# Moving the gates' small operations from the second expert's step to the end of the first expert's up-projection

## The chip, the cores and the metric

One core of one Trainium2 chip runs the program. The metric is the device time of one execution in microseconds (us). The kernel before takes 889.69 us, the median of three runs (887.64, 889.69 and 891.66).

## What is computed

One layer of a decoder trunk on 512 tokens of width 1024: an HGRN2 branch and a stick-breaking attention branch, mixed; a cross-attention to a memory of 256 rows; and a mixture of experts. Each of the three ends in a residual and a layer norm. All is float32 at the outside. The change lies in the last stage, the mixture of experts:

```python
g_prob = softmax(hf @ wg + bg);  g_top, g_idx = top_k(g_prob, 1)        # 1 of 4 groups
in_group = the 4 expert logits of that group
e_top, e_idx = top_k(softmax(in_group), 2)                              # 2 of 4 experts
gate_w = g_top * (e_top / sum(e_top))
for e in range(16):
    hidden = silu(hf @ w1[e]) * (hf @ w3[e])                            # 1024 -> 512
    y += combine[:, e:e+1] * (hidden @ w2[e])                           # 512 -> 1024
out = layer_norm(alpha * h + y)
```

`combine` holds `gate_w` at a token's two experts and zero elsewhere.

## The kernel before

**Stages.** The first two thirds of the span compute the two branches and the cross-attention, with float32 products split in three. The mixture of experts runs from about 596 us on. It does not multiply every token with every expert: the router gives each expert a list of slots, and each expert's weights (two of 1024 x 512 and one of 512 x 1024, 6.3 MB) are streamed once.

**One expert's step.** The loop over `e` issues, in this order: `up(e)`, the first two products for 64 slots, whose two halves run side by side in TensorE's columns (L1425), and a conditional part for slots 64 to 127 (L1412 to L1415, L1436), which TensorE's sequencer enters only if the count of tokens, loaded into a register at L1430, is over 64 or 96; `turn_in(e + 1)`, eight transposes (L1398) of the next expert's token rows, with two copies out of PSUM (L1399); the start of the gather for expert `e + 3` (L1161, on POOL's queue); for `e > 0` the second product of expert `e - 1`, `down(e - 1)` (L1466, with its own conditional part), the scaling of its result by the slots' gates in `to_rows` (L1489, L1495 on ScalarE, L1497 on VectorE), and the scatter that adds the rows to the sum in memory (L1273, POOL's queue); and `turn_hidden(e)`, four transposes of the hidden rows (L1453). Expert 0's second product is thus issued in the step of expert 1.

**Weights.** `Weights` (`W`) keeps a list of loads of 512 KB each, in order of use, and the free buffers. `W.done(j)` frees a buffer and at once issues the next load on SP's queue (L54); SP waits there until the buffer's last reader is through. In `up`, `W.done` stands behind the conditional part, so the eight buffers of an `up` are free for SP when TensorE's sequencer has passed the If at L1412. Buffers for some 40 loads make the stream run ahead of TensorE.

**Side work.** `begin(gen, wait)` puts a generator on a list; `tick()`, called after every pair of weights, lets it issue a part of its instructions once its waiting time is used up, and `finish()` issues all that is left. `tell()` (L1362) is begun before the loop and finished in `up(0)`: it counts the tokens, tells each slot its token (L1109, with one-hot matrices), starts the gathers for experts 1 and 2, and issues the first half of the gates' chain (`route_gates`, L1119: five VectorE operations, then two exponentials on ScalarE, L1133 and L1134). `tell_gates()` (L1375) is the rest: `route_gates_rest` with 12 small VectorE operations (L1139 to L1153), 24 bf16 products of 128 x 16 that sum each slot's gate (L1109) into the PSUM tile `told`, a copy (L1380), ten float32 products, 20 TensorE instructions (L1385), that move the gates to the partitions in which `to_rows` wants them, and a copy to `gates_at` (L1386). Before the change it is begun in step 0, behind `turn_in(1)`, so it is issued in the ticks of `up(1)` and of `down(0)`. `gates_at` is read first by `to_rows(0)`, at the end of `down(0)`.

Every engine works through its instructions in the order of issue.

Of the kernel before, what the change touches and what calls it, by code (L numbers as in the profile page):

```python
# [96 lines left out]
def tile_kernel(ctx, tc, x, mem, ln_in_g, ln_in_b, w_in, hg_lb_logits, hg_norm_g, w_branch_a, w_branch_b,  # L97
# [51 lines left out]
    def work(name, shape, dt=F32, bufs=2):  # L149
        return pp.tile(shape, dt, tag=name, bufs=bufs, name=nc.get_next_instruction_name() + name)  # L150
# [47 lines left out]
    def tick(n=1.0):  # L198
        for s in list(side):
            s[1] -= n  # L200
            while s[1] <= 0:
                try:
                    s[1] += next(s[0]) or 1
                except StopIteration:
                    side.remove(s)
                    break

    def begin(gen, wait=0):
        side.append([gen, wait])

    def finish(gen=None):
        while side:
            tick()
# [892 lines left out]
    def sums(o, items):  # L1106

        for i, (r, t, k) in enumerate(items):
            nc.tensor.matmul(o, oh_b[r][:, t], C[:, k, r, t], start=i == 0, stop=i == len(items) - 1)  # L1109
# [27 lines left out]
    def route_gates_rest():  # L1137
        L, top, tmp = logits, gexp[:, :, 4], gexp[:, :, 0:4]
        nc.vector.tensor_reduce(gates[:, 0, 0], tmp, op=ALU.add, axis=AX.X)  # L1139
        yield 0.35  # L1140
        nc.vector.scalar_tensor_tensor(gates[:, 0, 0], gates[:, 0, 1], 1.0, gates[:, 0, 0], op0=ALU.add, op1=ALU.mult)
        yield 0.35
        nc.vector.reciprocal(gates[:, 0, 0], gates[:, 0, 0])
        yield 0.35
        nc.vector.tensor_tensor(gates[:, 0, 1], gates[:, 0, 0], gates[:, 0, 1], op=ALU.mult)
        yield 0.35
        f = lambda x: x.rearrange("p r t -> p (r t)")
        for i in range(3):
            part = gparts[:, i]
            nc.vector.tensor_copy(part, f(gates[:, i]))  # L1150
            if i < 2:
                nc.vector.tensor_tensor(f(gates[:, i + 1]), f(gates[:, i]), part, op=ALU.subtract)
            nc.vector.tensor_tensor(C[:, 2 + i].rearrange("p r t e -> p (r t) e"), m.rearrange("p r t e -> p (r t) e"),  # L1153
                                    part[:, :, None].to_broadcast([P, 2 * NT, NE]), op=ALU.mult)
            yield 0.35
# [4 lines left out]
    def gather(e):  # L1160
        nc.gpsimd.indirect_dma_start(out=gx[e % 2], out_offset=None, in_=x2d[:, :],  # L1161
                                     in_offset=bass.IndirectOffsetOnAxis(ap=gidx[:, e:e + 1], axis=0),
                                     bounds_check=T - 1, oob_is_err=False)
# [101 lines left out]
    def more_blocks():  # L1265
        n = nc.values_load(more[0:1, 8:9], min_val=0, max_val=7)
        with tc.If(n > 0):
            list_blocks()
            with tc.For_i(0, n):
                one_block()  # L1270

    def scatter(y, idx):
        nc.gpsimd.indirect_dma_start(out=yd[:, :], out_offset=bass.IndirectOffsetOnAxis(ap=idx, axis=0),  # L1273
                                     in_=y, in_offset=None, bounds_check=T - 1,
                                     oob_is_err=False, compute_op=ALU.add)
# [99 lines left out]
    def tell_gates():  # L1375
        yield 0.5
        yield from route_gates_rest()
        yield 2
        sums(told[:, NE:2 * NE], [(r, t, k) for r, t in all_rt for k in range(2, 5)])
        nc.vector.tensor_copy(gate, told[:, NE:2 * NE])  # L1380
        yield 1

        for i, (s0, n) in enumerate(((0, 64), (64, 32), (96, 32))):
            for k in range(0, P, n):
                nc.tensor.matmul(told[k:k + n, (i + 2) * NE:(i + 3) * NE], ident[:, s0:s0 + n], gate, start=True, stop=True)  # L1385
        nc.vector.tensor_copy(gates_at, told[:, 2 * NE:5 * NE].rearrange("p (a e) -> p a e", e=NE))  # L1386
# [6 lines left out]
    def turn_in(e):  # L1393
        xg = gx[e % 2].rearrange("t (q p k) -> t q k p", q=4, k=2)
        for q in range(2):
            p = msp()
            for i in range(4):
                nc.tensor.transpose(p[:, i * P:(i + 1) * P], xg[:, 2 * q + i // 2, i % 2], ident)  # L1398
            (nc.scalar.copy, nc.vector.tensor_copy)[q](xgT[:, e % 2, 4 * q:4 * q + 4],  # L1399
                                                       p.rearrange("p (k n) -> p k n", n=P))  # L1400
# [9 lines left out]
    def further(e, part):  # L1410
        n = beyond[e]
        with tc.If(n > 64):  # L1412
            part(0)
            with tc.If(n > 96):
                part(1)  # L1415

    def up(e):
        x, (a, b) = xgT[:, e % 2], sums_up
        ws = []
        for q, js in enumerate(q_up[e]):  # L1420
            ws.append([W.get(j) for j in js])
            for k in range(2):
                c = 2 * q + k
                for i, w in enumerate(reversed(ws[q])):
                    nc.tensor.matmul(a[64 * i:64 * i + 64], x[:, c, 0:64], w[:, k * 512:(k + 1) * 512], start=c == 0,  # L1425
                                     stop=c == 7)
            tick()
        if e == 0:
            finish()
        beyond[e] = nc.tensor.value_load(tally[0:1, e:e + 1], min_val=0, max_val=T)  # L1430

        def part(g):
            for c in range(8):
                for i in range(4):
                    o = c % 2 * 512 + i % 2 * 256
                    nc.tensor.matmul(b[32 * i:32 * i + 32, 256 * g:256 * g + 256],  # L1436
                                     x[:, c, 64 + 32 * g:96 + 32 * g], ws[c // 2][i // 2][:, o:o + 256],
                                     start=c == 0, stop=c == 7)

        further(e, part)  # L1440
        for js in q_up[e]:
            for j in js:
                W.done(j)
        h = work("w2k", [P, T], bufs=5)
        for s, gated, other in ((slice(0, 64), a[64:128], a[0:64]), (slice(64, 128), b[0:64], b[64:128])):
            nc.scalar.activation(h[s], gated, AF.Silu)
            nc.vector.tensor_tensor(h[s], h[s], other, op=ALU.mult)
        return h

    def turn_hidden(e, h, p=None):  # L1450
        p = p or msp()
        for i in range(4):
            nc.tensor.transpose(p[:, i * P:(i + 1) * P], h[:, i * P:(i + 1) * P], ident)  # L1453
        x = work("w2k", [P, T], bufs=5)
        nc.vector.tensor_copy(x, p)  # L1455
        hT[e] = x.rearrange("p (k n) -> p k n", n=P)

    def down(e):

        x, (a, b) = hT.pop(e), sums_down  # L1460
        ws = [W.get(j) for j in q_w2[e]]

        def base():
            for k, w in enumerate(ws):
                for n in range(2):
                    nc.tensor.matmul(a[64 * n:64 * n + 64], x[:, k, 0:64], w[:, n * 512:(n + 1) * 512], start=k == 0,  # L1466
                                     stop=k == 3)
                tick()

        def part(g):  # L1470
            for k, w in enumerate(ws):
                s = slice(64 + 32 * (k // 2), 96 + 32 * (k // 2))
                for i in range(4):
                    nc.tensor.matmul(b[32 * i:32 * i + 32, 256 * g:256 * g + 256], x[:, 2 * g + k % 2, s],
                                     w[:, 256 * i:256 * i + 256], start=k == 0, stop=k == 3)

        def rest():
            further(e, part)
            for j in q_w2[e]:
                W.done(j)  # L1480

        return base, rest
# [17 lines left out]
    for e in range(NE - 1):  # L1500
        h = up(e)
        turn_in(e + 1)
        if e + 3 < NE:
            gather(e + 3)
        if e == 13:
            scratch.extend(W.raw_free.pop() for i in range(4))
            more_blocks()
            W.buffers(scratch)
        if e == 0:
            begin(tell_gates())  # L1510
        if e > 0:
            for step in down(e - 1):
                step()
            finish()
            scatter(to_rows(e - 1), gidx[:, e - 1:e])
        turn_hidden(e, h)
# [58 lines left out]
    ident_r = pp.tile([P, 3 * P], F32R, tag="hgc", name="ident_r")[:, 0:P]  # L1575
    nc.scalar.copy(ident_r, ident)
    h = up(NE - 1)
    for t in (1, 2):
        split_tile(t, rooms.pop())
# [115 lines left out]
```

## Time and profile before

| | |
|---|---|
| median of three runs | 889.69 us |
| profiled execution, whole | 890.44 us |
| its span | 888.3 us |
| TensorE matmul busy (PE) | 846.5 us, 95% |
| TensorE weight load busy (PEld) | 585.1 us, 66% |
| VectorE (DVE), ScalarE (ACT), GpSimd (POOL) busy | 458.7, 337.2, 128.4 us |
| moved by DMA | 177.65 MB, 200 GB/s on the mean |

In the profile's second part the span is cut in 40 slices of 22.2 us. From the 27th slice to the 38th (577 to 844 us) the DMA engines are busy nine tenths or more, at 343 to 389 GB/s, and TensorE eight to nine tenths. The matmuls' ends are modelled, so a busy TensorE need not be at its peak. The releaser that a view names for an idle time is inferred from semaphore events. "PEq", "SPq" and "POOLq" are the engines' sequencers, which take instructions from the program and wait on semaphores.

### The profile page before, as it was taken

To read this page: it belongs to the slowest core of one execution; us is meant where nothing else is said; L and a number is where in the kernel's file an instruction comes from. 1 tells how busy PE (TensorE), PEld (TensorE's weight loads), DVE (VectorE), ACT (ScalarE), POOL (GpSimd) and SP (SyncE) were. 2 spreads that over 40 slices of the span, in tenths; PEclk is the share of its full clock that TensorE was granted. 3 is DMA by queue.
4 is the path that set the end of the run, shared out by engine and by line. 5 is a ranking of instruction groups with operands and counts; after the bars stand their busy time and mean duration, and the time that the engine had idled before them with its cause. 6 is when DMAs were issued, how large, how long until landed. Compare 5 with 4: busy or idle time off the path is not lost. (4 is left out here: it accounts for less than half of the span.)

```text
span 888.3 us, 13677 instructions
## 1 busy us (share of the span) xinstructions
PE 846.5 (95%) x5296; PEld 585.1 (66%) x5296; DVE 458.7 (52%) x804; ACT 337.2 (38%) x640; POOL 128.4 (14%) x214
## 2 busy tenths in 40 slices
PE   6999999999999999999999999998989999889994
PEld 5887777788777777887988888763333433334343
DVE  6632577644657554759844566684232323322346
ACT  3332336542554544412533444322333323323234
POOL 5300000000212220004200000221121211110102
PEclk8999999999999999999999999999999999999998
DMA  8433232223212225331852567599999999999942
GB/s 305 151 116 95 74 95 72 72 72 96 72 48 80 87 99 211 136 101 48 241 166 71 194 217 277 202 355 366 389 368 358 343 357 353 352 350 377 372 168 95
DMA packets 63907, 177.65 MB, mean 200 GB/s; under 512 B 7797, under 2 KB 7829, under 8 KB 63824
## 3 DMA queue, kind: packets, MB, share of 16 engines
q1 hardware_dynamic: 56144, 157.31, 49.4%
q0 software_dynamic: 7536, 18.65, 6.9%
q8 instruction: 60, 0.98, 0.4%
q10 hardware_dynamic: 144, 0.52, 0.1%
q14 instruction: 23, 0.19, 0.1%
HBM read 168.47 MB, written 15.73 MB: 207 GB/s over the span
## 5 line engine op out<-in xcount | busy, mean ns | idle before, releaser
L1497 DVE TENSOR_SCALAR ringgb<-I-5389_acc,wgb 32x256 f32<-32x256 f32 x60 | 29.2, 487 | 123.6 <-ACT ringgb L1495 122.2
L1425 PE MATMUL I-5383_acc<-ring,xgT 128*64 128x512 f32 x284 | 78.3, 599 | 1.8 <-DMA ring<-in_moe_w_dram 1.8
L1489 ACT ACTIVATE ringgb<-I-5387_acc,wgb 64x512 f32<-64x512 f32 x30 | 20.5, 683 | 86.5 <-DMA yd<-ringgb,s 67.0
L67 DVE TENSOR_TENSOR I-69_out<-raws,I-69_out 128x1024 fp32r<-128x1024 f32 x24 | 29.3, 1222 | 38.2 <-ACT I-69_out L65 37.9
L1273 POOL DMA_INDIRECT yd<-ringgb,s x14 | 22.4, 1597 | 169.3 <-DVE I-8217w2k L1455 18.0
L1425 PEld LDWEIGHTS I-5383_acc<-ring,xgT 128*64 128x64 f32 x284 | 23.5, 138 | 35.3 <-issue 33.9
L663 DVE TENSOR_TENSOR_SCAN wx<-sbk 128x128 f32<-128x128 f32 (+3 forms) x32 | 27.1, 847 | 28.7 <-POOL sbk L659 28.7
L65 ACT CAST I-73_out<-raws 128x1024 fp32r<-128x1024 f32 x23 | 24.2, 1050 | 46.2 <-PE I-3563_acc L190 17.1
L67 DVE TENSOR_TENSOR I-71_out<-raws,I-71_out 128x1024 fp32r<-128x1024 f32 x22 | 26.9, 1222 | 24.7 <-ACT I-71_out L65 24.6
L65 ACT CAST I-69_out<-raws 128x1024 fp32r<-128x1024 f32 x25 | 26.3, 1050 | 32.7 <-issue 9.2
L65 ACT CAST I-71_out<-raws 128x1024 fp32r<-128x1024 f32 x24 | 25.3, 1055 | 24.9 <-PE I-384_acc L189 4.6
L67 DVE TENSOR_TENSOR I-73_out<-raws,I-73_out 128x1024 fp32r<-128x1024 f32 x21 | 25.7, 1222 | 16.1 <-ACT I-73_out L65 15.8
L1425 PE MATMUL I-5383_acc<-raws,xgT 128*64 128x512 f32 x64 | 30.7, 615 | 0.0
L1495 ACT ACTIVATE ringgb<-I-5389_acc,wgb 32x256 f32<-32x256 f32 x60 | 27.8, 464 | 4.3 <-issue 2.2
L659 POOL TENSOR_SCALAR_AFFINE_SELECT sbk<-sbk 128x128 f32<-128x128 f32 x32 | 14.3, 447 | 94.5 <-ACT sbk L654 50.2
L1436 PE MATMUL I-5385_acc<-ring,xgT 128*32 128x256 f32 x408 | 26.4, 380 | 0.0
L1436 PEld LDWEIGHTS I-5385_acc<-ring,xgT 128*32 128x32 f32 x408 | 14.1, 110 | 13.8 <-issue 4.9
L216 POOL TENSOR_TENSOR I-1461hgss<-I-1461hgss,mhalf 128x4 f32<-128x4 f32 x1 | 1.0, 1047 | 136.9 <-DVE I-1461hgss L567 136.9
L1425 PE MATMUL I-5383_acc<-ringout,xgT 128*64 128x512 f32 x80 | 17.9, 595 | 0.0
L940 POOL MEMSET I-4802w2k<- 128x128 f32 x1 | 0.2, 204 | 109.9 <-PE I-4748_ms L190 109.9
L1425 PEld LDWEIGHTS I-5383_acc<-raws,xgT 128*64 128x64 f32 x64 | 8.5, 142 | 8.3 <-issue 7.6
L1425 PEld LDWEIGHTS I-5383_acc<-ringout,xgT 128*64 128x64 f32 x80 | 5.6, 137 | 10.6 <-issue 10.6
(3489 smaller groups left out, 2404.4 us busy)
## 6 DMA issues: line engine op xcount, KB each, us to landing
ring<-in_moe_w_dram SPq DMA_DIRECT2D x114, 512.0 KB, 12.5
raws<-in_w_in_dram SPq DMA_DIRECT2D x44, 512.0 KB, 3.5
ringout<-in_moe_w_dram SPq DMA_DIRECT2D x32, 512.0 KB, 12.6
raws<-in_moe_w_dram SPq DMA_DIRECT2D x20, 512.0 KB, 11.1
xres<-in_moe_w_dram SPq DMA_DIRECT2D x16, 512.0 KB, 13.3
raws<-in_xa_wk_dram SPq DMA_DIRECT2D x7, 512.0 KB, 3.6
raws<-in_xa_wv_dram SPq DMA_DIRECT2D x7, 512.0 KB, 4.2
raws<-in_w_mix_out_dram SPq DMA_DIRECT2D x6, 512.0 KB, 4.9
```

The source lines that it names most:

```text
L65: self.nc.scalar.copy(hi, raw)
L67: eng.tensor_tensor(lo, raw, hi.bitcast(F32), op=ALU.subtract)
L216: nc.gpsimd.tensor_tensor(o, v, mhalf[:, :v.shape[-1]], op=ALU.pow)
L659: nc.gpsimd.affine_select(kp[:, d], kp[:, d], pattern=[[-1, P]], compare_op=ALU.is_gt, fill=1.0, base=w * (P - 1), channel_multiplier=1 - ...
L663: nc.vector.tensor_tensor_scan(rest[:, :n][:, ::-1], kp[:, n:0:-1], kp[:, n:0:-1], 1.0, ALU.mult, ALU.bypass)
L940: nc.gpsimd.memset(wsum[0][:, 0:P], 1.0)
L1273: nc.gpsimd.indirect_dma_start(out=yd[:, :], out_offset=bass.IndirectOffsetOnAxis(ap=idx, axis=0), in_=y, in_offset=None, bounds_check=T - ...
L1425: nc.tensor.matmul(a[64 * i:64 * i + 64], x[:, c, 0:64], w[:, k * 512:(k + 1) * 512], start=c == 0, stop=c == 7)
L1436: nc.tensor.matmul(b[32 * i:32 * i + 32, 256 * g:256 * g + 256], x[:, c, 64 + 32 * g:96 + 32 * g], ws[c // 2][i // 2][:, o:o + 256], start ...
L1489: nc.scalar.activation(y[0:64, n * 512:(n + 1) * 512], a[s], AF.Copy, scale=gates_at[s, 0, e:e + 1])
L1495: nc.scalar.activation(o, z, AF.Copy, scale=f)
L1497: nc.vector.tensor_scalar(o, z, f, None, op0=ALU.mult)
```

## The change

In `up`, behind `finish()` for expert 0, all of `tell_gates()` is issued at once, ahead of the load of the count (L1430), the conditional part, `W.done` and `turn_in(1)`. The `begin(tell_gates())` in step 0 goes, so the ticks of `up(1)` and `down(0)` issue nothing beside. The instructions themselves are the same.

```diff
@@ up(e)
         if e == 0:
             finish()
+            for _ in tell_gates():
+                pass
         beyond[e] = nc.tensor.value_load(tally[0:1, e:e + 1], min_val=0, max_val=T)
@@ for e in range(NE - 1)
             more_blocks()
             W.buffers(scratch)
-        if e == 0:
-            begin(tell_gates())
         if e > 0:
             for step in down(e - 1):
                 step()
```

## Rows read from the trace of the kernel before

**Rows 1.** Busy time by stretch: PE, PEld, DVE, ACT, POOL, granted clock, DMA share, GB/s.

```profile
604.00:605.30 1.30, 0.01 (x2) 0.00 (x0) 0.61 (x1) 1.18 (x2) 0.00 (x0) 1.00 1.09 410
605.30:607.20 1.90, 0.00 (x0) 0.00 (x0) 0.76 (x2) 0.00 (x0) 0.00 (x0) 1.00 1.01 365
607.20:616.00 8.80, 8.67 (x38) 4.04 (x40) 3.42 (x14) 0.58 (x1) 0.98 (x1) 0.81 1.03 404
616.00:617.80 1.80, 1.63 (x8) 0.28 (x4) 0.00 (x0) 0.07 (x1) 0.00 (x0) 1.00 0.62 244
617.80:624.00 6.20, 6.05 (x68) 3.09 (x68) 2.44 (x5) 1.70 (x3) 0.99 (x1) 1.00 0.80 275
624.00:628.00 4.00, 3.84 (x22) 1.62 (x22) 0.49 (x2) 3.22 (x6) 0.00 (x0) 1.00 1.02 404
...
640.00:780.00 140.00, 129.86 (x836) 52.02 (x830) 42.32 (x72) 45.08 (x82) 23.80 (x18) 1.00 0.98 357
```

**Rows 2.** TensorE's timeline: start, us, operation, idle time before it and releaser.

```profile
607.33 0.74 PE L1398 MATMUL I-5542_ms<-ident,ringgb 128*128 128x128 f32 x4 [3.32 <-DMA ringgb<-x2d,s]
...
620.09 0.76 PE L1109 MATMUL I-5359_ms<-s,I-5372w2k 128*128 128x16 bf16 x24
...
621.68 0.49 PE L1385 MATMUL I-5359_ms<-s,ident 128*64 128x16 f32 x20
...
782.25 1.94 PE L1425 MATMUL I-5383_acc<-ring,xgT 128*64 128x512 f32 x8 [1.76 <-DMA ring<-in_moe_w_dram]
```

**Rows 3.** What SP's queue waited for, 640 to 782 us: total us, times, longest.

```profile
SPq L54 <- DMA ring<-in_moe_w_dram: 61.8, 48, 3.1
...
SPq L54 <- PEq L1412: 1.3, 4, 0.4
```

**Rows 4.** SP's timeline: loads issued, merged.

```profile
607.25 10.85 SPq L54 DMA_DIRECT2D ring<-in_moe_w_dram  x4
```

**Rows 5.** Busy time by stretch: transposes, products and an idle stretch of TensorE.

```profile
607.33:617.63 10.30, 10.30 (x44) 4.32 (x44) 3.42 (x14) 0.58 (x1) 0.98 (x1) 0.83 0.97 382
617.95:624.05 6.10, 6.09 (x68) 3.06 (x68) 2.44 (x5) 1.55 (x3) 0.99 (x1) 1.00 0.81 279
632.16:633.28 1.12, 1.12 (x8) 1.00 (x8) 0.73 (x2) 1.07 (x3) 0.00 (x0) 1.00 1.02 399
637.10:644.75 7.65, 7.64 (x36) 2.59 (x36) 1.67 (x4) 3.22 (x6) 0.00 (x0) 1.00 1.04 408
633.28:636.94 3.66, 3.66 (x17) 1.06 (x16) 1.34 (x2) 0.44 (x1) 1.05 (x1) 1.00 1.03 372
659.10:661.30 2.20, 0.05 (x2) 0.03 (x1) 2.07 (x5) 1.11 (x2) 0.05 (x1) 1.00 0.93 331
```

**Rows 6.** VectorE's timeline: the gates' chain and the first copy.

```profile
601.98 0.22 DVE L1131 TENSOR_REDUCE s<-rw 128x4 f32<-128x64 f32 x1
...
610.56 0.16 DVE L1141 SCALAR_TENSOR_TENSOR s<-s 128x4 f32<-128x4 f32 x1
...
612.35 0.29 DVE L1153 TENSOR_TENSOR s<-s 128x128 bf16<-128x128 f32 x1
...
620.88 0.17 DVE L1380 COPY s<-I-5359_ms 128x16 f32<-128x16 f32 x1 [0.40 <-PE I-5359_ms L1109]
```

**Rows 7.** ScalarE's timeline: the second exponential.

```profile
602.23 0.20 ACT L1134 ACTIVATE s<-s 128x4 f32<-128x4 f32 x1 [0.43 <-DVE s L1131]
```

**Rows 8.** TensorE's sequencer, L1430, 600 to 602 us: ns min/median/max, first and last start.

```profile
L1430 PEldq TENSOR_LOAD <-s x1: 494/494/494, 600.4 to 600.4; - x1
```

**Rows 9.** TensorE's sequencer, L1412: two rows of expert 0, and all branches.

```profile
L1412 PEldq COMPARE_BRANCH  x1: 364/364/364, 601.3 to 601.3; - x1
...
L1412 PEldq EVENT_SEMAPHORE  x1: 51/51/51, 604.1 to 604.1; - x1
...
L1412 PEldq COMPARE_BRANCH  x31: 65/318/1832, 601.3 to 854.5; - x31
```

**Rows 10.** DMA in 605.3 to 607.2 us, by queue: packets, MB, share of 16 engines.

```profile
q0 software_dynamic: 191, 0.28, 39.3%
```

## The prediction

> **What bounds the kernel now.** I read four views, in this order. First the busy times by stretch over the expert stage [rows 1]: from 640 to 780 us the DMA engines are 98% busy while TensorE, by its modelled ends, is busy 129.86 of 140 us. Two resources are near their limits, so the question is which one the other waits for. Second, TensorE's timeline [rows 2]: there the reader is to see two places. At 604.01 us, with expert 0's up-projection done, TensorE stands idle 3.32 us for the gather of expert 1's rows. At 782.25 us it has been idle 1.76 us for a load of weights: by then it has used up the whole lead of the weight stream. Third, what SP's queue waits for [rows 3]: between 640 and 782 us it waits 61.8 us, 48 times, for loads under way into the ring alone, and only 1.3 us, four times, for TensorE to pass an If. So buffers are free and the stream runs as fast as the DMA engines let it. From these two I take it that the load awaited at 782 us sets the time there, and TensorE everything after it: what TensorE gains before 782 us it stands idle for, unless the stream comes earlier too. The fourth view shows whether that can be, since the stream has one hole [rows 1]. From 616.0 to 617.8 us the DMA engines move 244 GB/s and from there to 624.0 us 275, against 404 beside it. The hole has a cause [rows 4]: the last of SP's four merged issues goes out only at its end, 618.1 us, and the queue had nothing left in the meantime; it waited for the buffers of expert 1's up-projection, and ran slow after it began again.
>
> **The change, part by part.**
>
> *Expert 0's second product gets shorter.* 24 sums (0.76 us) and 20 products (0.49 us) leave it [rows 2]. The stretch from expert 2's transposes through that product takes 6.10 us; the same work one expert later takes 1.12 + 3.66 = 4.78 us [rows 5]. That is 1.32 us less on TensorE's path.
>
> *The chain goes into the gap.* VectorE is through with the chain's first half at 601.98 + 0.22 = 602.20 us [rows 6], ScalarE with the second exponential at 602.43 us [rows 7]. From the operation that needs it to the end of the chain took 612.64 - 610.56 = 2.08 us [rows 6]; started at 602.5 us it ends at 604.6 us. The sums then take 0.76 us, to 605.35; the copy with its hand-over 0.2 (0.17 the copy itself [rows 6]), to 605.55; the products 0.49, to 606.05 us [rows 2]. All of this lies inside the idle 3.32 us and costs nothing while the gather is out; without that cover it would cost TensorE the 2.0 us from 604.01 to 606.05. VectorE and ScalarE have nothing else to do there but expert 0's SiLU and its product, which queue behind the two copies and are wanted only after the eight transposes.
>
> *The register load and the branch come into the open.* Before, TensorE's sequencer took them at 600.4 and 601.3 us, ahead of products that the array was still working on until 604.0 [rows 8, 9]. Now they stand behind instructions that wait for VectorE. From the load's start to the branch's end took 601.3 + 0.36 - 600.4 = 1.26 us; from 606.05 that gives 607.3 us, and transposes at 607.4 against 607.33 before. Cost 0.1 us on TensorE. From below: if the load is taken as soon as the products are issued and hides behind them, nothing. From above: the longest branch of the 31 took 1.83 us instead of 0.36 [rows 9], which makes 1.5 us more. I take the value of expert 0's own branch, since it is the same branch.
>
> The Trainium skill speaks against that choice ("Runtime: NRT & Kernel Launch", Instruction fetch mechanics): a taken branch whose target is outside the window of code that the sequencer holds has to fetch it before it goes on, and the moved instructions change where this branch lies in the code. The trace has both kinds, a median of 0.32 us and one of 1.83 us [rows 9]; by the rule the long one may now fall on expert 0.
>
> *TensorE's clock.* It is granted 0.83 on the mean in the 10.30 us after the gap [rows 5], that is partly at 1.2 GHz instead of 2.4. The same transposes and products at full clock take 1.12 + 7.65 = 8.77 us, so the low clock costs 1.53 us. Before it fell TensorE had been idle 3.32 us; after the 2.20 us at 659.10 us, nearly all idle, the next matmuls still ran at 1.00 [rows 5]. The gap is now broken up, with no idle piece over 1.35 us. I take the whole 1.53 us as gained; the other end is nothing.
>
> So TensorE reaches the end of expert 0's second product 1.32 + 1.53 - 0.1 = 2.75 us earlier (1.2 if the clock falls all the same).
>
> *The release of the buffers.* This is the part that I think decides. The eight buffers of expert 0's up-projection are handed to SP when the If has been passed: 604.1 us before [rows 9], 607.3 us now. Until then SP stands still, and nothing else is on its queue; the gathers on POOL's queue were issued earlier. How much did the stream have left at 604.1? From there to 616.0 us the rows give 1.3 x 410 + 1.9 x 365 + 8.8 x 404 GB/s = 4.78 MB [rows 1], and the eight loads are 4.19 MB; with 0.28 MB of gathers [rows 10] little is left, an estimated 0.3 to 0.5 MB, about one load. So the stream now runs dry at about 605.3 us and begins again at 607.3. In exchange the hole at 616 us closes: 4.19 MB started at 607.3 us last, with the slow start of 6.2 us at 275 GB/s (1.70 MB) and the rest at 404, to 607.3 + 6.2 + 6.2 = 619.7 us, and expert 1's buffers come back at 616.4 us (617.9 if the clock falls), before that.
>
> The sum, bytes moved from 604.0 to 628.0 us. Before: 0.53 + 0.69 + 3.56 + 0.44 + 1.70 + 1.62 = 8.54 MB [rows 1]. Now: 0.53 until 605.3, 0.28 of gathers, 1.70 in the slow start until 613.5, 14.5 us x 404 = 5.86, together 8.37 MB. The stream is 0.17 MB behind, 0.4 us at 404 GB/s. Bounds: with the load and the branch hidden the release comes at 606.1 us and the stream is 0.8 us ahead; with the long branch, 1.9 us behind.
>
> **Forecast.** The hole moves from 616 us to 605 us and costs as much as before. The end follows the stream: 890.44 + 0.4 = 890.8 us for the profiled execution, which lies 0.75 us above the median of the runs, so 890.1 us for the median; its own range is 888.9 to 891.3.
>
> **The rivals.**
>
> *TensorE is the bound.* The stream then has slack enough, and 2.75 us come through to the end: 890.44 - 2.75 - 0.75 = 886.9 us. For it: one wait of 1.76 us is all that I can show for the stream, and without the profiler's own traffic there may be none. Against it: the 98% in 140 us and SP's waits. A weaker form, in which the clock falls all the same, gives 1.2 us: 888.5 us.
>
> *Slower, by the branch.* Expert 0's branch takes the long time. Transposes start at 608.8 us instead of 607.33, the buffers are released at 608.8, and the stream ends 1.9 us behind: 890.44 + 1.9 - 0.75 = 891.6 us. For it: one branch of the 31 took that long, and this one stands where the code now moves. Against it: half of them took 0.32 us or less. Its point of decision is a release at 606.9 us, where the new hole costs what the closed one gives back; each microsecond behind that costs about one, and the full price needs the 1.83 us.
>
> **How the numbers follow.** Forecast 0.46, TensorE as the bound 0.26, its weaker form 0.08, the slow branch 0.16, none of these 0.04. The range takes in the first rival and the second with the spread of a median: 886.3 to 892.4 us. A change by 0.5%, 4.4 us, is about what a measurement of this kernel can tell from none; none of the cases reaches it, so I leave 0.07 on either side, for what I have not seen, and 0.86 for no change.
>
> **What would show it.** In the profile of the changed kernel: sums at about 604.6 us and products by 606.1 us in the gap; transposes within 0.2 us of 607.4; a granted clock of 1.00 in the up-projection behind them, and its end near 616.4 us; expert 0's second product in 3.7 us; SP's first load of the next eight at 607.3 us, GB/s low from 605.3 on and full at 616 to 624 us; and a longer wait for weights where experts 10 and 11 stand, by about the 2.75 us that TensorE gained and the 0.4 us that the stream lost. The prediction is wrong if that wait does not grow and the end comes earlier by 2 us or more, or if the hole of the stream at 616 us stays beside the new one.

## The result: slower, 895.65 us beside 890.07

The changed kernel takes 895.65 us, the median of six runs (891.12 to 896.85), beside 890.07 for the kernel before in six runs (887.64 to 891.66). The ratio is 1.0061, 95% interval [1.0045, 1.0077]: slower by 0.6%, clear of the spread of the runs. The forecast was 890.1 us with a range of 886.3 to 892.4, and the measured median lies above it. The profiled execution took 896.43 us with a span of 894.2. Line numbers behind L1430 are two higher than before (the register load is L1432, the second product L1468).

TensorE's timeline of the changed kernel (start, us, operation, idle time before it and releaser), the rows that answer to [rows 2] and three more:

```profile
604.35 0.70 PE L1109 MATMUL I-5359_ms<-s,I-5372w2k 128*128 128x16 bf16 x22 [0.24 <-DVE s L1153]
605.31 0.54 PE L1385 MATMUL I-5359_ms<-s,ident 128*64 128x16 f32 x20 [0.27 <-DVE s L1380]
609.99 1.10 PE L1398 MATMUL I-5590_ms<-ident,ringgb 128*128 128x128 f32 x4 [4.13 <-PEq L1412]
...
622.46 3.65 PE L1468 MATMUL I-5387_acc<-ring,I-5613w2k 128*64 128x512 f32 x16
...
663.50 5.07 PE L1468 MATMUL I-5387_acc<-ring,I-6183w2k 128*64 128x512 f32 x16 [2.28 <-issue]
...
785.85 1.94 PE L1425 MATMUL I-5383_acc<-ring,xgT 128*64 128x512 f32 x8 [1.65 <-DMA ring<-in_moe_w_dram]
...
814.72 0.72 PE L1398 MATMUL I-7991_ms<-ident,wx 128*128 128x128 f32 x4 [1.30 <-issue]
...
816.31 5.35 PE L1468 MATMUL I-5387_acc<-ringout,I-7891w2k 128*64 128x512 f32 x16 [0.39 <-DMA ring<-in_moe_w_dram]
```

The chain and the products are done at 605.85 us, 0.2 ahead of the forecast. Then the reader is to see a gap of 4.13 us that ends with PEq, TensorE's own sequencer, at L1412: expert 0's branch. The sequencer's rows of that line (ns min/median/max, first and last start), beside [rows 9]:

```profile
L1412 PEldq COMPARE_BRANCH  x1: 3350/3350/3350, 606.5 to 606.5; - x1
L1412 PEldq EVENT_SEMAPHORE  x1: 51/51/51, 609.9 to 609.9; - x1
```

The branch took 3.35 us instead of 0.36, and all this time in the open. What hung on it: the transposes came 2.66 us late, and SP's next load was issued at 609.96 us instead of 604.15. SP's timeline, and below it what its queue waited for from 640 to 782 us (columns as in [rows 3]):

```profile
609.96 0.33 SPq L54 DMA_DIRECT2D ring<-in_moe_w_dram  x1
```

```profile
SPq L54 <- DMA ring<-in_moe_w_dram: 60.1, 48, 3.5
```

Behind 640 us SP waits for loads under way as before [rows 3]: the DMA engines are full again, so most of what was lost is not made good (of the 4.3 us that the table below gives for 640 us, 3.6 are left at 785.85). Busy time by stretch, columns as in [rows 1]:

```profile
604.00:606.00 2.00, 1.34 (x43) 1.05 (x42) 0.54 (x3) 0.29 (x1) 0.00 (x0) 1.00 0.78 301
606.00:610.00 4.00, 0.01 (x1) 0.05 (x1) 0.72 (x2) 0.04 (x1) 0.00 (x0) 0.80 0.11 40
610.00:616.00 6.00, 6.00 (x22) 3.44 (x24) 2.08 (x3) 1.14 (x2) 0.99 (x1) 0.57 0.79 268
616.00:618.00 2.00, 2.00 (x12) 0.70 (x10) 0.00 (x0) 0.00 (x0) 0.00 (x0) 1.00 1.02 402
618.00:624.00 6.00, 5.69 (x32) 2.37 (x28) 2.06 (x3) 1.77 (x3) 0.99 (x1) 1.00 1.02 393
```

The stream of weights stands still from 606 to 610 us (40 GB/s) and starts again slowly (268). The hole at 616 us is closed, as forecast, but the new one is far larger. The granted clock in expert 1's up-projection is 0.57 from 610 to 616 us: it did not stay at 1.00.

The wait for weights at 785.85 us is as long as before (1.65 beside 1.76 us [rows 2]) and 3.60 us later. By the count of transposes this is expert 12's up-projection; the expectations below call the place expert 11. Behind it, expert 12's second product adds the rest: transposes 0.5 us later behind a longer gap, and 5.35 us for a product that takes 3.65 elsewhere.

### The profile page after: what moved, and what is told of

It reads as the page before. It is cut to its first block, busy times and chain, and to the rows that moved or that the text cites. A ratio compares the mean times of both kernels' runs of the same rounds, so it can differ in the third digit from the quotient of the medians.

```text
span 894.2 us, 13680 instructions
## 1 busy us (share of the span) xinstructions
PE 850.8 (95%) x5296; PEld 586.3 (66%) x5296; DVE 458.7 (51%) x804; ACT 337.1 (38%) x640; POOL 128.4 (14%) x214
## 5 line engine op out<-in xcount | busy, mean ns | idle before, releaser
L1161 POOL DMA_INDIRECT ringgb<-x2d,s x8 | 8.4, 1046 | 31.7 <-PE I-5597_ms L1398 9.2
```

## The experiments

Four theories of the loss stood against each other: the branch's code fetch (A; A2 if it hangs on the place of its target in the code, A1 if any branch in the open costs it) and the moved chain itself (B), as its origin; the late stream of weights (S) and TensorE's own lateness (P), as the way in which it reaches the end.

One table serves all of them. Release: the start of SP's first load behind expert 0. Turn: the first transposes of expert 1. GB/s: what the DMA engines moved from 600 to 640 us; "stream" is what it is behind the kernel before, (373 - GB/s) x 40 us / 404 GB/s. The two shifts are those of the transposes that stand at 755.65 us (ahead of the wait for weights) and 793.62 us (behind it) in the kernel before. Profiled: time of the profiled execution less 890.44. All columns but the last two come from that one execution, in which the expert stage can itself begin a little earlier or later (products that stand at 585.54 us in the kernel before stand 1.02 us earlier in e8 and 1.27 later in e3). Each ratio is to the runs of the kernel before on the same chip. All in us but GB/s and the ratio.

| kernel | release | turn | GB/s | stream | shift at 756 | shift at 794 | profiled | median | ratio to before |
|---|---|---|---|---|---|---|---|---|---|
| before | 604.15 | 607.33 | 373 | 0 | 0 | 0 | 0 | 890.07 | 1 |
| changed | 609.96 | 609.99 | 330 | 4.3 | 3.70 | 3.59 | 5.99 | 895.65 | 1.0061 [1.0045, 1.0077] |
| e1 | 604.20 | 607.49 | 377 | -0.4 | -0.38 | -0.71 | -0.56 | 890.78 | 1.0007 [0.9994, 1.0019] |
| e2 | 610.28 | 610.31 | 342 | 3.1 | 1.50 | 2.89 | 3.88 | 894.53 | 1.0051 [1.0036, 1.0067] |
| e3 | 605.43 | 608.63 | 388 | -1.5 | -0.66 | -0.12 | -0.30 | 890.41 | 1.0005 [0.9995, 1.0015] |
| e4 | 609.78 | 607.38 | 333 | 4.0 | 0.16 | 2.88 | 2.96 | 892.84 | 1.0034 [1.0020, 1.0049] |
| e5 | 604.10 | 614.81 | 303 | 6.9 | 9.77 | 6.77 | 10.63 | 899.02 | 1.0102 [1.0076, 1.0128] |
| e6 | 607.67 | 607.70 | 362 | 1.1 | 1.00 | 1.62 | 3.43 | 892.16 | 1.0040 [1.0021, 1.0059] |
| e7 | 606.30 | 607.83 | 370 | 0.3 | 0.53 | -0.72 | 5.14 | 894.56 | 1.0052 [1.0031, 1.0072] |
| e8 | 606.29 | 606.49 | 347 | 2.6 | 2.17 | 2.32 | 2.27 | 893.50 | 1.0049 [1.0031, 1.0067] |
| e9 | 609.92 | 609.95 | 342 | 3.1 | 1.72 | 1.96 | 2.09 | 892.53 | one run |
| e10 | 603.92 | 607.21 | 381 | -0.8 | -2.31 | -1.08 | -1.27 | 890.56 | 1.0001 [0.9990, 1.0012] |
| e11 | 608.30 | 608.33 | 359 | 1.4 | 1.93 | 2.28 | 2.01 | 893.26 | 1.0038 [1.0024, 1.0051] |

**e1: the same chain, ahead of the turning, but behind the branch and the buffers' return.**

```diff
-            for _ in tell_gates(): ...      # ahead of the load of the count
 ... conditional part, W.done ...
+        if e == 0:
+            for _ in tell_gates(): ...
         turn_in(e + 1)
```

> tell_gates is issued in up(0) behind the conditional part and the handing back of the buffers, still ahead of the transposes. Theory A (the branch in the open): what cost the time is that the register load and the branch of expert 0 stood behind the gates' chain; put back ahead of it, the branch takes 0.4 us under running products, SP issues its next load at 604.2 us, the transposes start at 607.3 to 607.6 us, the clock stays at 1.00, expert 1's up-projection ends at 616.4 and expert 0's second product at 621.4 us. If the weight stream sets the end, it gains the 1.5 us by which expert 1's buffers come earlier: 887 to 889.5 us. Theory B (the chain): 44 small operations that wait for VectorE do harm wherever they stand ahead of the transposes; then the time stays at 894 to 897 us.

TensorE's timeline in e1, sums to transposes, and its wait behind 780 us:

```profile
605.72 0.46 PE L1385 MATMUL I-5359_ms<-s,ident 128*64 128x16 f32 x6 [0.27 <-DVE s L1380]
607.25 0.31 PE L1385 MATMUL I-5359_ms<-s,ident 128*32 128x16 f32 x14 [1.07 <-issue]
607.49 1.13 PE L1398 MATMUL I-5590_ms<-ident,ringgb 128*128 128x128 f32 x4
...
781.52 1.94 PE L1425 MATMUL I-5383_acc<-ring,xgT 128*64 128x512 f32 x8 [1.56 <-DMA ring<-in_moe_w_dram]
```

The branch is quick (0.367 us at 601.3), the release on time, the loss gone. So the moved work costs nothing: where it stands relative to the branch does. TensorE stops for 1.07 us in the middle of the products, waiting for nothing recorded. The hoped-for 1.5 us did not come.

**e2 and e3: fewer warm-up products (`WARM = 14` to `8`, ahead of 10 us), in the changed kernel and in the one before.** TensorE's code moves by 24 instructions; the order of the work stays.

> The changed kernel with 8 warm-up products instead of 14 at the start, which moves all later code of TensorE 24 instructions forward, so that the target of expert 0's branch comes 24 instructions earlier. Theory A1 (place in the code): the 3.35 us were a fetch of a block of code in which the target lay; with the target before the block's edge the branch takes 0.3 to 0.5 us, the transposes start at 607.2 to 607.5 us, SP's next load goes out at 607.1 us, and the time is that of the prediction, 889 to 891.5 us. Theory A2 (any branch in the open): a branch with no products queued ahead of it takes 3 us wherever it lies, and the time stays at 894 to 897 us.

> The kernel before with 8 warm-up products instead of 14: the control for the run with the changed kernel. All theories: within 1 us of the kernel before, 889 to 891 us, up to 1 us more if the clock is low for longer at the start; expert 0's branch takes 0.3 to 0.5 us, hidden.

In e2 the branch still takes 3.33 us. The run doesn't decide what it was made for: the target, 24 places earlier, may still lie behind the same edge. In e3 expert 0's branch stays quick (0.368) but expert 1's takes 3.51 us, where the kernel before has none over 1.83 [rows 9]: the price wanders with the place in the code. There the products hide it.

**e4: the kernel before, with only SP's eight loads held back.** A small transfer that has to wait for the turned tokens is put on SP's queue ahead of them.

```diff
+            nc.sync.dma_start(hold, xgT[:, 1, 7, 124:128])
+            for js in q_up[0]: ...  W.done(j)
```

> The kernel before, but SP's next eight loads wait behind a transfer of 2 KB that reads the copied transposes of expert 1, so they go out at about 609.6 us instead of 604.15; TensorE's order is that of before. Theory S (the stream sets the end): the DMA engines run dry from 605.5 to 611 us as in the changed kernel, TensorE keeps its times until it waits for weights at expert 11's up-projection, that wait grows from 2.3 to 5 or 6 us, and the end comes 3 to 4 us later: 893 to 894.5 us. Theory P (TensorE sets the end): a stream that is late by 5 us early on is hidden by its lead, and the time stays within 1 us of 890.

TensorE's timeline in e4:

```profile
766.24 1.94 PE L1425 MATMUL I-5383_acc<-ring,xgT 128*64 128x512 f32 x8 [1.28 <-DMA ring<-in_moe_w_dram]
...
775.41 5.35 PE L1467 MATMUL I-5387_acc<-ring,I-7515w2k 128*64 128x512 f32 x15 [2.72 <-issue]
...
787.58 0.64 PE L1425 MATMUL I-5383_acc<-s,xgT 128*64 128x512 f32 x1 [0.53 <-DMA s<-in_moe_w_dram]
```

TensorE keeps its time to 0.2 us for 150 us, and then meets weights that are not there, 1.28 us and, at 768.67, another 0.49, where the kernel before waits for none. The late release alone, with no late TensorE, costs 2.9 us, 2.8 by the medians on this chip. Not all of it is a wait for weights: behind 771 us a longer gap and a slower product (5.35 instead of 3.65 us) make TensorE 4.6 us late, and the wait of 1.76 us that the kernel before has at 782.25 [rows 2] is no longer there. So e4 shows what the late release costs, but not that the awaited load sets the time at 782 us; e10 below shows that.

**e5: the release on time, TensorE late.** e1 with nine round trips between TensorE and VectorE behind the chain.

```diff
+            for _ in range(9):
+                nc.tensor.matmul(told[:, NE:2 * NE], ident, gate, start=True, stop=True)
+                nc.vector.tensor_copy(gate, told[:, NE:2 * NE])
```

> Buffers handed back on time, TensorE late: the order of e1 (chain and products behind expert 0's conditional part and its buffers' return, so that SP's next load is issued at about 604.2 us), and then nine round trips between TensorE and VectorE (gates multiplied by the identity matrix, copied back) ahead of the turning of expert 1's tokens. Each trip should cost about 0.3 us, so the first of these transposes comes near 610 instead of 607.5, as late as in the changed kernel. If the stream of weights sets the end (theory S), TensorE runs some 2.5 us late up to expert 11, its waits for weights there shrink from 2.1 us to nothing or nearly, and the time is 890 to 891.5. If TensorE's own lateness is what cost the changed kernel its 5.6 us (rival P), the waits at expert 11 move with it and the time is 893 to 896.

The clock fell during the round trips, a trip took 0.87 us and the delay was 7.5 us, not 2.5. SP's timeline and two stretches of e5:

```profile
607.28 18.64 SPq L54 DMA_DIRECT2D ring<-in_moe_w_dram  x4
```

```profile
616.00:618.00 2.00, 2.00 (x10) 1.37 (x10) 1.49 (x3) 0.53 (x1) 0.97 (x1) 0.50 0.38 150
618.00:624.00 6.00, 6.00 (x26) 1.78 (x24) 0.42 (x1) 0.00 (x0) 0.02 (x1) 0.90 0.14 37
```

Neither theory had this: a TensorE that is late enough returns expert 1's buffers late, and the stream stops for that (37 GB/s). The two can't be parted beyond the lead that the buffers give. The test failed as a contrast at 2.5 us; it shows the other half of the loop.

**e6 and e7: the code moved the other way.** 80 tiny products behind the first warm-up (160 instructions of TensorE) in the changed kernel, 44 (88 instructions, as many as the change puts ahead of the branch) in the kernel before.

```diff
+    tiny = ident.bitcast(BF)
+    for i in range(80):                     # 44 in e7
+        nc.tensor.matmul(warm[:, 0:16], tiny[:, 0:P], tiny[:, 0:16], start=True, stop=True)
```

> The changed kernel with 80 small products (160 instructions of TensorE, 16 columns each) added behind the first warm-up of the program, in an idle stretch of TensorE before 10 us: nothing else moves, but every later instruction of TensorE stands 160 places further in the code. If the 3.35 us of expert 0's branch are the fetch of its target's code, which lies just behind an edge of a code block when the branch is reached (theory A2), the branch now finds its target fetched: 0.3 to 0.5 us in place of 3.35, the transposes near 607.3, SP's next load near 607.1 and a time of 889 to 891.5, as I had forecast for the change. If any branch that TensorE reaches in the open costs 3 us here, wherever its target lies (rival A1), the branch stays at about 3.3 us, the transposes at 610, and the time is 894 to 897.

> The kernel before with 44 small products (88 instructions of TensorE) added behind the first warm-up, before 10 us: the branch of expert 0 then stands at the place in the code that it has in the changed kernel, and nothing is moved. Theory A2: the branch, reached at about 603.8 us, now takes about 3.3 us instead of 0.36; the buffers of expert 0's up-projection come back at about 607.2 instead of 604.1, the transposes hardly move (607.3 to 607.7, they wait for the gather until 607.3 anyway), TensorE keeps its time up to expert 10, and the waits for weights at expert 11 grow by 0.5 to 2 us: 890.5 to 892. Rival A1: the branch stays at 0.36 us and the time at 889.5 to 890.5.

Expert 0's branch (L1412, here L1415) in e6, then in e7:

```profile
L1415 PEldq COMPARE_BRANCH  x1: 358/358/358, 607.2 to 607.2; - x1
```

```profile
L1415 PEldq COMPARE_BRANCH  x1: 4456/4456/4456, 601.7 to 601.7; - x1
```

This settles the branch. In e6 the same order of work has a branch of 0.36 us, a release at 607.67 and transposes at 607.70, near where the forecast had them (607.3 and 607.4). In e7 the old order has one of 4.46 us, more than half of it hidden behind products that the array still had until 604.4 us. It is the place in the code, neither the chain nor a branch in the open as such. The place does not fix the price: e7's branch stands where the changed kernel's does and takes 1.1 us longer.

Neither time is the expected one, and one place accounts for most of that. TensorE's timeline at expert 12's second product, in e6 and then in e7; its normal form is 3.65 us behind a wait of 0.4:

```profile
815.56 3.65 PE L1471 MATMUL I-5467_acc<-ringout,I-7971w2k 128*64 128x512 f32 x16 [2.34 <-PEq L1270]
```

```profile
814.55 6.42 PE L1469 MATMUL I-5431_acc<-ringout,I-7935w2k 128*64 128x512 f32 x16 [3.68 <-PEq L1270]
```

The shift made another branch (L1270, ahead of a scatter) take the long time, 4.00 us in e7, with nothing left behind it to absorb it, and in e7 the product behind it takes 6.42 us instead of 3.65: past the last wait for weights every microsecond counts. e7 is 0.7 us ahead at 794 us and 5.1 behind at the end.

**e8: five warm-up products in the changed kernel (36 instructions fewer).**

> The changed kernel with 5 in place of 14 warm-up products (36 instructions fewer, before 10 us): the target of expert 0's branch comes to lie a few instructions ahead of the code block's edge instead of behind it. Theory A2: the branch is quick (0.3 to 0.5 us), the buffers come back near 607, and TensorE then stops at the edge, a few instructions on, for the code that the branch used to wait for: transposes near 609 to 610. So the release is late by 2.8 us and TensorE by 2 to 2.5. By the stream (theory S) the time is 891 to 893; by TensorE's lateness (rival P) 892.5 to 894.5. Rival A1: the branch stays at 3.3 us and the time at 894 to 896.

```profile
606.49 0.97 PE L1398 MATMUL I-5581_ms<-ident,ringgb 128*128 128x128 f32 x4 [1.30 <-DMA ringgb<-x2d,s]
609.30 1.01 PE L1398 MATMUL I-5588_ms<-ident,ringgb 128*128 128x128 f32 x4 [1.84 <-issue]
```

With 12 instructions fewer than e2 the branch is quick (0.358 us) and the stop comes a few instructions on, between two groups of transposes. That is an edge in the code, by the count of instructions and by a packet of code (see below) that starts 2.41 us before TensorE goes on. The profiled execution gives 892.7, the median 893.5 us. That does not part theory S from rival P, since TensorE and the stream are late by about the same (2.2 and 2.6 us in the table).

**e9 to e11: the changed kernel once more; e1 with 8 warm-up products; the changed kernel with 20 tiny products.**

> The changed kernel itself, looked at once more. In its first profile 3.6 us of the 5.9 at the end stand in the wait for weights at expert 11, and a further 2.2 us come at expert 12 (transposes 1.30 us behind a code fetch, 814.72, and a second product of 5.35 in place of 3.65 us at a granted clock of 0.68 for that stretch). If the first part is the buffers' late return (theory S), it is there again: branch of expert 0 at 3 to 3.6 us, SP's next load at 609.5 to 610.5, transposes of expert 12's successor stage at the wait of expert 11 later by 3 to 4 us. If the second part is not a fixed cost of the order but depends on where the clock stands in an execution (theory C), it differs: the second product of expert 12 takes 3.65, or another product is slow instead. If it is fixed (rival F), it is 5.3 to 5.4 again.

> The order of e1 (chain and products behind expert 0's conditional part and its buffers' return) with 8 in place of 14 warm-up products, which moved e3's code edge and left the clock at full speed behind the gap there, so that by 628 us the stream had moved 0.6 MB more (1.5 us at 404 GB/s). If order and code place add up: transposes of expert 2 near 630.7 (e1: 630.92), the stream 0.3 to 1.5 us ahead of that of before at 640 us, the end 0.5 to 1.5 us earlier: 888.5 to 889.7 beside 890. Rival: the clock falls behind the gap as in e1, and the time is 889.8 to 891.

> The changed kernel with 20 small products (40 instructions of TensorE) added behind the first warm-up, before 10 us. The code block's edge then lies 57 instructions ahead of expert 0's branch instead of 17, among the chain's sums, and TensorE passes it near 604.8 us instead of 605.6. If passing an edge is what asks for the next block, and that block is there 3.2 to 4.3 us later (3.15 us in the kernel before, 4.25 in the changed one, both from the edge to the branch's end), the branch ends at 608.0 to 609.1: 1.3 to 2.5 us in place of 3.35, SP's next load at 608.1 to 609.2, and by 640 us the stream is 2 to 3 us late: 891.5 to 893.5. If the branch itself asks for its target (rival), it stays at 3.3 us and 894 to 896.

Expert 0's branch in e9 and in e11:

```profile
L1412 PEldq COMPARE_BRANCH  x1: 3331/3331/3331, 606.5 to 606.5; - x1
```

```profile
L1415 PEldq COMPARE_BRANCH  x1: 1331/1331/1331, 606.8 to 606.8; - x1
```

TensorE's timeline in e9, ahead of the wait for weights and at it, and then in e10:

```profile
774.58 5.12 PE L1468 MATMUL I-5387_acc<-ring,I-7513w2k 128*64 128x512 f32 x15 [1.87 <-issue]
...
784.21 1.94 PE L1425 MATMUL I-5383_acc<-ring,xgT 128*64 128x512 f32 x8 [0.16 <-DMA ring<-in_moe_w_dram]
```

```profile
780.35 3.50 PE L1425 MATMUL I-5377_acc<-ring,xgT 128*64 128x512 f32 x8 [3.55 <-DMA ring<-in_moe_w_dram]
```

e9 has the same branch, release and transposes as the first profile, but the end is 2.1 us late instead of 6.0. The second part of the loss is not fixed: the products at 663 and 816 us take 3.65 us each, and another is slow instead (774.58), where the wait for weights takes it up. Nor is the first part: behind that wait TensorE is 1.96 us late, not the expected 3 to 4. The stream was 3.1 us behind by 640 us instead of 4.3. From 613 to 616 us the granted clock was 0.88 instead of 0.63, and SP could go on behind expert 1's buffers at 620.83 instead of 621.58 us.

e11 gives an intermediate branch, 1.33 us, within the forecast from where the edge is passed (its stream is 1.4 us behind by 640 us, not 2 to 3). A packet of code starts 0.99 us before this branch, so something ahead of the branch had asked for it, and the branch waited for what was left.

e10 takes 2.3 us off TensorE's path as far as 756 us, and the wait for weights grows from 1.76 us [rows 2] to 3.55: what TensorE gains it stands idle for. The load comes 1.9 us earlier, but the eight products behind the longer wait take 3.50 us instead of 1.94. The median does not move: 890.56, ratio 1.0001.

## Why the prediction was wrong, by its steps

**The step that failed is "the register load and the branch come into the open".** Its cost was put at 0.1 us, with 1.5 us more as the end of the range, since the longest branch in the trace took 1.83 us [rows 9]. It took 3.35 us. The register load was as forecast (0.50 us). That expert 0's branch had taken 0.36 us was no property of the branch: it was the state of the code fetch when it was reached. The traces show how: code arrives in single packets on a queue of its own, of which the page of the changed kernel counts 60:

```profile
q8 instruction: 60, 0.98, 0.4%
```

That is 16 KB each. In the changed kernel one starts at 607.49 us, and the branch ends at 609.82. In e11 it is 605.85 and 608.17; in e7 603.75 and 606.17; in e1, at the stop among the products, 604.87 and 607.25. From the start of the packet to progress it is 2.3 to 2.4 us each time. This is no selection: of the 754 branches of TensorE in the thirteen traces 46 took over 0.9 us, and 45 of these ended 2.3 to 2.6 us behind the start of such a packet. The row of 1.83 us from which the prediction took its bound is one of them:

```profile
L1412 PEldq COMPARE_BRANCH  x1: 1832/1832/1832, 613.9 to 613.9; - x1
```

Its packet had started at 613.35 us, 0.55 us before the branch. The longest row was thus the rest of a fetch already under way, and no bound for a whole one: in the changed kernel the packet starts only 1.02 us behind the start of the branch.

The change puts 88 instructions (24 sums, 20 products, a weight load for each) ahead of the branch. By a count of the code, which no view shows, TensorE then enters a block only some 17 instructions before the branch and jumps into the next. Before, by the same count, the jump went into a block whose packet had come at 591.66 us, and the next packet, at 604.83 us, was hidden behind the gather, which ended at 607.33 [rows 2].

The Trainium skill's rule that the prediction weighed and left aside ("Runtime: NRT & Kernel Launch", Instruction fetch mechanics: blocks of 16 KiB, 256 instructions, fetched in sequence; a taken branch out of the held window waits for its code) fits these branches. Its remark that the crossing of an edge is mostly hidden does not hold at two places here: e1 and e8 stop 1.07 and 1.84 us at one.

**The rival "slower, by the branch" had the mechanism and a third of the price.** It put the stream 1.9 us behind, of the 5.99 measured, for 891.6 us; the size of the branch, taken from the longest row, was the term that was too small. With the release at 609.9 instead of 608.8 us and one microsecond for each, its own rule gives 1.9 + 1.1 = 3.0 us, and e4 measures 2.9 for that release. The rest of the 5.99 us is in neither the forecast nor this rival: slow products, of which more below.

**"The stream sets the end": right where it can be read.** In the changed kernel TensorE waits 1.65 us for a load that comes 3.60 us later than before, and in e10 it gains 2.3 us and then stands idle 1.8 us longer for that load. Over all twelve kernels the shift at 794 us lies within 1.4 us of what the stream had lost by 640 us; for the changed kernel the two are 3.59 and 4.3 us. The shift at 756 us parts from the end in e4 (0.16) and e10 (-2.31), but in most kernels TensorE is late there by about as much as the stream. In e4, e5 and e11 TensorE comes to the place of the wait so late, by stops and slow products of its own, that it waits for no load there, so in these three the shift at 794 us is no reading of the stream. The forecast that the wait would grow failed, since TensorE was as late as the stream.

**The clock: wrong.** It was taken to stay at full speed once the gap was broken up (+1.53 us). The branch made a longer gap, so the changed kernel is no test; e6 is. There no idle piece of the gap is over 1.13 us and the granted clock falls all the same, to 0.82 from 611 to 616 us:

```profile
611.00:616.00 5.00, 5.00 (x20) 1.46 (x18) 0.00 (x0) 0.00 (x0) 0.00 (x0) 0.82 0.91 343
```

Nor does the length of the pause tell it: 607 to 611 us in e1 and e10, both behind a stop of 1.07 to 1.09 us:

```profile
607.00:611.00 4.00, 3.75 (x28) 2.83 (x29) 2.81 (x5) 0.59 (x1) 0.98 (x1) 0.58 0.96 391
```

```profile
607.00:611.00 4.00, 3.47 (x22) 2.19 (x23) 2.87 (x5) 0.59 (x1) 0.98 (x1) 1.00 1.00 404
```

The same pause, and 0.58 of full speed in one, 1.00 in the other. e3 has the gap of 3.33 us as in [rows 2] and stays at 1.00.

**Right as forecast:** the times of the chain, sums and products; 1.32 us off expert 0's second product (3.65 us for 16 products behind transposes that end at 622.5); the closing of the hole at 616 us. All of it came in where nothing waits for it.

**Where the 5.99 us of the profiled execution are.** 3.6 are the late stream, which TensorE meets at 785.85 us. Some 2.2 more come at expert 12, behind the last wait: 0.5 in the gap at 814.72 and 1.7 in a product at a granted clock of 0.68 (3.61 us of work in 5.29). The product at 663.50 us lost 1.4 us in the same way (granted clock 0.71), ahead of the wait for weights. In e9 neither product lost anything, and the late stream cost 1.96 us. So the slow branch is in both executions, and how much of the loss follows from it varies.

**Would the forecast have held with a quick branch?** Not quite. e6 takes 892.16 us: in its profiled execution the stream is 1.1 us late instead of 0.4, and the branch at L1270 adds 2. What e6 would take with no branch in a bad place anywhere was not tried.

**Open:** which executions see the clock fall, and why. The single run of e9 took 892.53 us and one of the six first runs 891.12; the other five, the profiled one among them, lie between 894.5 and 896.9. That the other four had clock drops like the profiled one is not shown: the mean granted clock does not sort them (0.988 in the run of 894.53 us, 0.986 in that of 891.12). Open too is what asks for a packet of code. In the changed kernel it starts behind the start of the branch, in e11 ahead of it; in e1, where the edge is passed at 607.25 us, the next packet comes only at 611.89.

## What to carry to other kernels

When instructions move across a branch, or simply come ahead of it, ask where the branch and its target will lie in the code and how long TensorE will have been in the block: a branch that is cheap in one trace costs 3 to 4 us in the next with no change in the work (e7: 44 tiny products 600 us earlier make the kernel 5.2 us slower). A branch's longest row in one trace is no bound for it: look whether its packet of code was already on the way. A branch that buffers wait behind belongs ahead of anything that stalls, as in e1, where the same move costs nothing. Before crediting or blaming a small edit on such a kernel, run it at two or three shifts of the code; and look for what lies behind the last wait for the bottleneck, since only there does a stall reach the end undiminished.

## What the runs showed of the hardware that was not expected

The branch of expert 0 on TensorE's sequencer took from 0.36 to 4.46 us for the same instruction when nothing but its place in the code and what stood ahead of it differed. A long branch ended 2.3 to 2.6 us behind the start of a packet of code, in 45 of 46; the packet itself started from 1.02 us (changed kernel) to 2.04 us (e7) behind the start of expert 0's branch, or before it (e11), and whether the weights on the same DMA engines held it up in e7 is not shown. The granted clock fell behind idle pieces of little over 1 us in some executions and stayed at 1.00 behind 3.33 us in another (e3). And the kernel's buffers couple the two engines in both directions: 5.6 us of late release cost 2.9 us with TensorE on time up to 756 us (e4), and 7.5 us of late TensorE emptied the stream with the release on time (e5).
